# Three of six early weight sums made in y's last places, rings that begin at free buffers, and last loads in places that y has left

## The chip, the cores and the metric

The kernel runs on one NeuronCore of one Trainium2 chip. The metric is the time of one execution on the device, in microseconds (us). Engines are named as in the profile: PE does matmuls and PEld loads their weights beside it, DVE is the vector engine, ACT the scalar engine, POOL the third elementwise engine, and SP issues most of the DMA transfers, in the order in which they stand on its queue.

## The reference, cut to what matters

The input has 256 tokens of 2048 channels. There is one layer (DEPTH is 1), so only the short convolution mixer is computed.

```python
def rmsnorm(x, g):
    y = x * lax.rsqrt(jnp.mean(x * x, axis=-1, keepdims=True) + EPS)
    return y * g

def adaln(h, c, w, b):
    mod = jnp.einsum('bd,df->bf', jax.nn.silu(c), w) + b
    shift, scale, gate = jnp.split(mod, 3, axis=-1)
    return h * (1.0 + scale[:, None, :]) + shift[:, None, :], gate

def short_conv_mixer(h, w_in, conv_w, w_out):      # w_in 2048 x 16384, w_out 4096 x 2048
    proj = jnp.einsum('bsd,de->bse', h, w_in)
    b_gate, c_gate, v, g = jnp.split(proj, 4, axis=-1)
    u = causal_depthwise_conv(c_gate * v, conv_w)   # width 3
    y = b_gate * u * jax.nn.silu(g)
    return jnp.einsum('bse,ed->bsd', y, w_out)

h, gate = adaln(rmsnorm(x, norm_g), c, ada_w, ada_b)
x = x + gate[:, None, :] * short_conv_mixer(h, w_in, conv_w, w_out)
out = rmsnorm(x, final_g)
```

## The kernel before, in words

Everything is float32. A product of two float32 matrices is made of three matmuls on PE: each operand is split into a rounded part `hi` and the rest `lo`, and hi times hi, hi times lo and lo times hi are summed. So every piece of weights goes the same way: a DMA brings it into a buffer `raw`, ACT rounds it into a buffer `hi` (L385), DVE subtracts to make `lo` (L390), and PE multiplies. A piece is 1 MB, 128 partitions of 2048 elements.

The buffers `raw`, `hi` and `lo` are three rings of three buffers each (`w_tile`, L146; `nth` counts where a ring stands). From the second matrix on, each ring has a fourth buffer for a while (`fourth`), a place that held something else before: for `lo` the place b0, for `hi` b1, for `raw` b2, and b2 held a part of `hT`, the normalised input that all matmuls of the first matrix read. A DMA into a buffer waits until the buffer's last reader has ended.

The stages, in the order of time:

- The head and the first half of the first matrix (banks `mm_s`), with the sums of ada_w between them, up to about 377 us.
- The second half of the first matrix (banks `mm_b`, the loop at L787): eight pairs of channel tiles, each by four quarters of two pieces, 64 pieces in all with 48 matmuls each (L550). In some places of this loop a piece of the second matrix is brought in ahead of its time (`early_weights`, L779). The table `EARLY` (L764) says after which piece: six "sums" units at 32, 36, 40, 44, 48 and 52, and two "gated" units at 56 and 60. A unit takes one buffer of the `raw` ring (`raw_u`, loaded at L757) and one of the `lo` ring (`sums_u`). For a sums unit DVE makes four sums of its blocks (L773, 776, 777), and ACT's queue stores the result to DRAM (`made`, L784) one piece later. POOL adds rows of the gate's sums (L719) up to about 610 us.
- The first columns of the second matrix, 16 pairs of row tiles (`first`, L1069). Pairs 8 to 15 go by seven products instead of eight, which need the sums of blocks: those made ahead are read from `made` into `sums_o`, the others are made by DVE here. A raw piece is now loaded into a buffer of the `lo` ring, and its `lo` goes into the `raw` ring, except that the very first piece still loads into the `raw` ring.
- The second columns (`second`), twelve pieces in the order 0, 1, 10, 2, 11, 3, 9, 12, 8, 13, 14, 15, of which 9 to 15 go by seven products. Beside them, the closing loads (`load_ends`, L862) and closing steps of the first columns.
- Four last pieces: the third quarter of the columns for two groups of rows (`third_piece`), and the two gated units read back (`gated_piece`). Then the end: norm, scaling and the store.

From L1063 on, all work stands in the order written, on every engine. In the loop at L787 a scheduler orders the work when the program is built, with some ties set by hand (`add_manual_dep`). `y`, the result between the two matrices, lies in 16 places of a pool of slots, y0 to y15, two channel tiles in each. y14 and y15 are written last.

Of the kernel before, what the change touches and what calls it, by code (L numbers as in the profile page):

```python
# [8 lines left out]
F32 = mybir.dt.float32  # L9
F32R = mybir.dt.float32r  # L10
# [3 lines left out]
P = 128  # L14
# [103 lines left out]
def short_conv_layer(ctx: ExitStack, tc: tile.TileContext, x, c, norm_g, ada_w, ada_b, w_in, conv_w, w_out, final_g, out):  # L118
# [256 lines left out]
    last_low = [None]  # L375

# [6 lines left out]
    def split_hi(raw, n, hi=None):  # L383
        hi = hi_tile() if hi is None else hi
        nc.scalar.copy(hi[:, :n], raw[:, :n])  # L385
        return hi
# [287 lines left out]
    ys.extend(slot([P, 2, 2, T], f"y{j}", F32R) for j in range(len(ys), NCT // 2))  # L674
# [5 lines left out]

    def gate_columns(c0, n):
        if c0 < D // 2:
            return closing[0][:, D // 2 + c0 : D // 2 + c0 + n]
        flat = gate_slots[0].rearrange("p h s f -> p (h s f)").bitcast(F32)
        return flat[:, c0 % 1024 : c0 % 1024 + n]
# [92 lines left out]

    def early_weights():  # L779

        while to_store:
            unit, sums = to_store.pop()
            made[unit] = dram.tile([P, SLOT], F32, tag=f"made{len(made)}", name="made")
            nc.scalar.dma_start(made[unit], sums)  # L784
        unit = EARLY.get(passed[0])
        passed[0] += 1
        if unit is None:  # L787
# [5 lines left out]
        raw, sums = raw_tile("raw_u"), w_tile("lo", "sums_u")  # L793
        blocks, out = (v.rearrange("p (b f) -> p b f", f=W) for v in (raw, sums))
        if unit[0] == "gated":
            load_o(raw, unit[1] * EP, EP, 3 * W, W)
            nc.vector.tensor_tensor(out=out, in0=blocks, in1=turned.unsqueeze(1).to_broadcast([P, EP, W]), op=ALU.mult)
# [64 lines left out]
    def load_ends(n):  # L862
# [20 lines left out]

# [30 lines left out]
    class Columns:  # L914
# [7 lines left out]
        def piece(self, n):  # L922
# [3 lines left out]
            raw = w_tile("raw" if n == 0 and c0 == 0 else "lo", "raw_o")  # L926
            ready = (c0, j) in made
# [26 lines left out]
        def seven(self, j, raw, sums, ready):  # L954
# [10 lines left out]
            opens, last = j == self.in_turn[0], j == self.in_turn[-1]  # L965

# [3 lines left out]
            def products():  # L970
# [3 lines left out]
                triple(p75[:, 0], f(2), sh[:, 1], sl[:, 1], opens, last)  # L974
                triple(p75[:, 1], f(0), sh[:, 0], sl[:, 0], opens, last)
# [43 lines left out]
    def third_piece(ep):  # L1019
        raw = w_tile("lo", "raw_o")  # L1020
        load_o(raw, ep * EP, EP, 2 * W, W)
        return ep, *split(raw, SLOT, "raw")
# [13 lines left out]

    def gated_piece(ep):
        raw = w_tile("lo", "raw_o")
        nc.sync.dma_start(raw, made["gated", ep])
        return raw  # L1040
# [24 lines left out]
    with in_order():  # L1065
# [77 lines left out]
```

## Time and profile before

| | us |
|---|---|
| median of three runs | 902.74 (900.94 to 904.39) |
| the profiled execution | 904.34, of which its span is 902.5 |
| PE busy | 885.8 (98%), clock 0.998 |
| DVE busy | 703.0 (78%) |
| ACT busy | 492.9 (55%) |
| POOL busy | 91.6 (10%) |

A row of the timeline is: start, length, engine and line, operation, what it writes and reads, and in brackets how long the engine stood idle before it and what ended that. A row of the chain of waits is: start, share of the chain, what the chain was doing then. The rows of the DMA view are groups of transfers with their count, their size and the median time from issue to landing. Matmuls overlap in the pipeline, so starts and not lengths say how fast PE goes.

### The profile page before, as it was taken

To read this page: it belongs to the slowest core of one execution; us is meant where nothing else is said; L and a number is where in the kernel's file an instruction comes from. 1 tells how busy PE (TensorE), PEld (TensorE's weight loads), DVE (VectorE), ACT (ScalarE), POOL (GpSimd) and SP (SyncE) were. 2 spreads that over 40 slices of the span, in tenths; PEclk is the share of its full clock that TensorE was granted. 3 is DMA by queue.
4 is the path that set the end of the run, shared out by engine and by line. 5 is a ranking of instruction groups with operands and counts; after the bars stand their busy time and mean duration, and the time that the engine had idled before them with its cause. 6 is when DMAs were issued, how large, how long until landed. Compare 5 with 4: busy or idle time off the path is not lost.

```text
span 902.5 us, 16524 instructions
## 1 busy us (share of the span) xinstructions
PE 885.8 (98%) x6974; PEld 847.6 (94%) x6974; DVE 703.0 (78%) x697; ACT 492.9 (55%) x437; POOL 91.6 (10%) x108
## 2 busy tenths in 40 slices
PE   7999999999999999999999999999999999999996
PEld 4999999999999999999999999999999988888775
DVE  5889988889988867856975687686766589777996
ACT  6767966656558856644343443344434446455553
POOL 0000000010000224420043003310000000000000
PEclk9999999999999999999999999999999999999999
DMA  9999999999998597776877889999998575689672
GB/s 309 367 369 363 366 326 363 332 366 364 373 335 290 164 293 229 240 224 199 284 226 238 256 281 292 312 298 323 299 304 288 197 252 212 195 299 379 235 267 93
DMA packets 165017, 257.29 MB, mean 285 GB/s; under 512 B 7684, under 2 KB 106596, under 8 KB 162896
## 3 DMA queue, kind: packets, MB, share of 16 engines
q1 hardware_dynamic: 159824, 239.89, 80.0%
q0 software_dynamic: 3840, 7.94, 3.2%
q10 hardware_dynamic: 1280, 8.43, 2.3%
q8 instruction: 54, 0.88, 0.4%
q14 instruction: 19, 0.16, 0.0%
HBM read 237.86 MB, written 10.50 MB: 275 GB/s over the span
## 4 chain that ended last, share of the span: by engine, by line
PE 81%; DMA 9%; DVE 6%; ACT 2%; issue 2%; SPq 0%; ACTq 0%; DVEq 0%
PE mm_s L550 39%; PE mm_b L550 27%; PE mm_w L898 7%; PE mm L898 4%; DMA raw<-in_sc_w_in_dram 4%; PE mm_o L898 3%; DVE lo L390 3%; DMA at<-in_ada_w_dram 2%; DMA at_g<-in_ada_w_dram 2%; ACT hi L385 2%; DMA raw_u<-in_sc_w_out_dram 1%; DVE gacc L713 1%; DVE sums_o L773 0%; DVE sums_o L777 0%; DVE sums_o L776 0%
## 5 line engine op out<-in xcount | busy, mean ns | idle before, releaser
L550 PE MATMUL mm_b<-hT,hi 128*128 128x256 f32 x2048 | 348.4, 276 | 0.0
L550 PE MATMUL mm_s<-hT,hi 128*128 128x256 f32 x2048 | 336.3, 277 | 0.0
L550 PEld LDWEIGHTS mm_b<-hT,hi 128*128 128x128 f32 x2048 | 308.2, 188 | 0.0
L550 PEld LDWEIGHTS mm_s<-hT,hi 128*128 128x128 f32 x2048 | 299.7, 188 | 0.2
L550 PE MATMUL mm_b<-hT,lo 128*128 128x256 f32 x1024 | 282.9, 276 | 1.5 <-DVE lo L390 1.5
L550 PE MATMUL mm_s<-hT,lo 128*128 128x256 f32 x1024 | 261.7, 277 | 0.0
L385 ACT CAST hi<-raw 128x2048 fp32r<-128x2048 f32 (+1 forms) x66 | 123.8, 1875 | 187.4 <-PE mm_b L550 88.9
L550 PEld LDWEIGHTS mm_b<-hT,lo 128*128 128x128 f32 x1024 | 192.2, 188 | 1.9 <-DVE lo L390 1.9
L390 DVE TENSOR_TENSOR lo<-raw,hi 128x2048 fp32r<-128x2048 f32 (+1 forms) x66 | 149.4, 2266 | 55.2 <-ACT hi L385 52.9
L550 PEld LDWEIGHTS mm_s<-hT,lo 128*128 128x128 f32 x1024 | 182.7, 188 | 0.0
L390 DVE TENSOR_TENSOR lo<-raw_s,hi 128x2048 fp32r<-128x2048 f32 (+1 forms) x80 | 148.2, 1860 | 29.6 <-ACT hi L385 29.1
L385 ACT CAST hi<-raw_s 128x2048 fp32r<-128x2048 f32 (+2 forms) x81 | 124.1, 1542 | 67.6 <-PE mm_s L550 42.7
L520 DVE SCALAR_TENSOR_TENSOR gv<-at,silu_c,gv 128x512 f32<-128x512 f32 x105 | 78.8, 751 | 9.4 <-DMA at<-in_ada_w_dram 7.5
L573 ACT COPY acc<-mm_s 128x1024 f32<-128x1024 f32 x54 | 54.7, 1012 | 29.6 <-PE mm_s L550 29.5
L719 POOL TENSOR_TENSOR gacc<-gacc,z 128x512 f32<-128x512 f32 x28 | 46.6, 1663 | 113.9 <-DMA z<-gacc 113.9
L898 PE MATMUL mm_w<-hi,y 128*128 128x512 f32 x160 | 52.1, 389 | 0.0
L713 DVE SCALAR_TENSOR_TENSOR gacc<-at_g,silu_c,gacc 128x512 f32<-128x512 f32 x60 | 45.0, 749 | 6.9 <-DMA at_g<-in_ada_w_dram 5.8
L385 ACT CAST hi<-sums_o 128x2048 fp32r<-128x2048 f32 x15 | 28.7, 1910 | 35.6 <-DVE sums_o L777 21.4
L390 DVE TENSOR_TENSOR lo<-raw_o,hi 128x2048 fp32r<-128x2048 f32 x17 | 38.8, 2287 | 11.8 <-PE mm_b L550 6.5
L898 PE MATMUL mm_o<-hi,y 128*128 128x512 f32 x140 | 45.7, 390 | 0.0
L390 DVE TENSOR_TENSOR lo<-sums_o,hi 128x2048 fp32r<-128x2048 f32 x15 | 34.4, 2291 | 12.6 <-ACT hi L385 12.6
L385 ACT CAST hi<-raw_o 128x2048 fp32r<-128x2048 f32 x17 | 32.5, 1909 | 21.0 <-DMA raw_o<-in_sc_w_out_dram 9.2
(188 smaller groups left out, 756.3 us busy)
## 6 DMA issues: line engine op xcount, KB each, us to landing
raw<-in_sc_w_in_dram SPq DMA_DIRECT2D x64, 1024.0 KB, 6.7
raw_s<-in_sc_w_in_dram SPq DMA_DIRECT2D x47, 1024.0 KB, 8.2
at<-in_ada_w_dram SPq DMA_DIRECT2D x126, 256.0 KB, 7.9
raw_o<-in_sc_w_out_dram SPq DMA_DIRECT2D x24, 1024.0 KB, 5.6
raw_s<-in_sc_w_in_dram SPq DMA_DIRECT2D x33, 512.0 KB, 7.4
at_g<-in_ada_w_dram SPq DMA_DIRECT2D x32, 512.0 KB, 8.4
raw_u<-in_sc_w_out_dram SPq DMA_DIRECT2D x8, 1024.0 KB, 5.4
made<-sums_u ACTq DMA_DIRECT2D x8, 1024.0 KB, 7.7
```

What stands on the lines that cost most here:

```text
L385: nc.scalar.copy(hi[:, :n], raw[:, :n])
L390: last_low[0] = nc.vector.tensor_tensor(out=lo[:, :n], in0=raw[:, :n], in1=hi[:, :n].bitcast(F32), op=ALU.subtract)
L520: nc.vector.scalar_tensor_tensor(out=gv, in0=at4[:, i], scalar=c_k, in1=gv, op0=ALU.mult, op1=ALU.add)
L550: mm = last_mm[0] = nc.tensor.matmul(dst, w, h[k], start=begins and left, stop=ends, skip_group_check=True)
L573: nc.scalar.copy(acc[ch, q], bank)
L713: nc.vector.scalar_tensor_tensor(out=ga, in0=at3[:, i, :], scalar=s, in1=ga, op0=ALU.mult, op1=ALU.add)
L719: nc.gpsimd.tensor_tensor(out=ga, in0=ga, in1=turned, op=ALU.add)
L898: nc.tensor.matmul(dst, y[a], b, start=opens and i == 0, stop=ends and i == 2, skip_group_check=True)
```

## The change

- **Units.** The sums for pair 13 of the first columns are no longer made ahead; those for pair 13 of the second columns are. The order of the six is now (0, 15), then 10, 11, 12, 13 and 15 of the second columns.
- **Three of the six in y's last places.** Units 0, 2 and 4 of that list, that is (0, 15), (1024, 11) and (1024, 13), no longer take a buffer of the rings. Each is loaded as two halves of 0.5 MB into the places of y14 and y15, which nothing uses yet. Four DVE operations of 512 columns make the sums in place, tied behind the `lo` of the next piece. Two stores of a half each follow three pieces after the load. Two of the four blocks come out in the other order, and `swapped` reads them so. To make this possible, every slot has its own tag, and y14 and y15 are allocated when they are first written. The other three sums units and the two gated units keep their buffers in the rings.
- **Rings.** At the first raw piece of the second matrix the counts of `raw` and `lo` are set to 0, so that the fourth buffer of `raw` (b2, with hT) is no longer the next one in turn.
- **Places.** x's second half goes to the places of y0 and y1, the gate's second half to that of y10. The third-quarter pieces are loaded as two halves each into y2 and y11, and y3 and y9, with their loads issued at pieces 8 and 11 of the second columns. The gated pieces go to y12 and y8, and y13 and y14. Each half is rounded and subtracted by an instruction of its own. A closing load moves from piece 9 to piece 10, and the closing steps come one piece later from piece 6 on.

```diff
-    slots = ctx.enter_context(tc.tile_pool(name="slots", bufs=NSLOT, side="right"))
-
-    def slot(shape, name, dtype=F32):
-        return slots.tile(shape, dtype, tag="slot", name=name)
+    slots = ctx.enter_context(tc.tile_pool(name="slots", bufs=1, side="right"))
+    taken = [0]
+
+    def slot(shape, name, dtype=F32, at=None):
+        if at is None:
+            at = taken[0] % NSLOT
+            taken[0] += 1
+        return slots.tile(shape, dtype, tag=f"slot{at}", name=name)
...
+    STAGES = 2
+    first_slot = taken[0] - len(ys)
+
+    def y_tile():
+        ys.append(slot([P, 2, 2, T], f"y{len(ys)}", F32R, at=(first_slot + len(ys)) % NSLOT))
+
+    while len(ys) < NCT // 2 - STAGES:
+        y_tile()
+    taken[0] = first_slot + NCT // 2
...
-    UNITS = ((0, 13), (0, 15), (2 * W, 10), (2 * W, 11), (2 * W, 12), (2 * W, 15))
+    UNITS = ((0, 15),) + tuple((2 * W, j) for j in (10, 11, 12, 13, 15))
     EARLY = {32 + 4 * i: unit for i, unit in enumerate(UNITS)}
+    IN_PLACE = UNITS[0:6:2]
     EARLY.update({55: "gate", 56: ("gated", LAST[0]), 60: ("gated", LAST[1])})
     made = {}
-    to_store = []
+    to_do = []
...
+    def sums_in_place(left, right):
+
+        low = last_low[0]
+        b0, b1, b2, b3 = left[:, 0], left[:, 1], right[:, 0], right[:, 1]
+        for out, a, b, op in (
+            (b1, b1, b0, ALU.subtract), (b0, b2, b0, ALU.subtract), (b2, b2, b1, ALU.add), (b3, b3, b2, ALU.subtract)
+        ):
+            step = nc.vector.tensor_tensor(out=out, in0=a, in1=b, op=op)
+            tc.add_manual_dep(step.ins, low.ins.name, after, reason="the blocks are there by then")
+
+    def store_made(unit, parts, turn=None):
+        made[unit] = dram.tile([P, SLOT], F32, tag=f"made{len(made)}", name="made")
+        n = SLOT // len(parts)
+        for i, made_part in enumerate(parts):
+            store = nc.scalar.dma_start(made[unit][:, i * n : (i + 1) * n], made_part)
+            if turn:
+                tc.add_manual_dep(store.ins, turn[0].ins.name, after, reason="the sums are there by then")
...
+        now = passed[0]
         passed[0] += 1
+        for due in [due for due in to_do if due[0] <= now]:
+            to_do.remove(due)
+            due[1](*due[2:])
...
+        if unit[0] == "gated" or unit not in IN_PLACE:
+            raw, result = raw_tile("raw_u"), w_tile("lo", "sums_u")
+            blocks, out = (v.rearrange("p (b f) -> p b f", f=W) for v in (raw, result))
+            if unit[0] == "gated":
+                load_o(raw, unit[1] * EP, EP, 3 * W, W)
+                nc.vector.tensor_tensor(out=out, in0=blocks, in1=turned.unsqueeze(1).to_broadcast([P, EP, W]), op=ALU.mult)
+            else:
+                load_o(raw, 2 * unit[1], 2, unit[0], 2 * W)
+                list(sums_of(blocks, out))
+            to_do.append((now + 1, store_made, unit, [result]))
         else:
-            load_o(raw, 2 * unit[1], 2, unit[0], 2 * W)
-            list(sums_of(blocks, out))
-        to_store.append((unit, sums))
+            c0, j = unit
+            parts = []
+            for i in range(STAGES):
+                parts.append(slot([P, 2 * W], "staged", at=(first_slot + NCT // 2 - STAGES + i) % NSLOT))
+                load = nc.sync.dma_start(parts[i], w_out[0, (2 * j + i) * P : (2 * j + i + 1) * P, c0 : c0 + 2 * W])
+                tc.add_manual_dep(load.ins, last_load[0].ins.name, after, reason="in its turn")
+            to_do.append((now + 1, sums_in_place, *(v.rearrange("p (b f) -> p b f", f=W) for v in parts)))
+            to_do.append((now + 3, store_made, unit, parts, last_high))
...
+                if len(ys) == ct // 2:
+                    y_tile()
...
-                xh.append([slot([P, HD], f"xr{t}") for t in range(TT)])
+                xh.append([y_place(j, f"xr{j}") for j in (0, 1)])
             load_x(1, n - 5)
         elif n == 7:
-            nc.sync.dma_start(gate_columns(HD, HD), gate_row[0:1, HD:D].partition_broadcast(P))
-        elif n == 9:
+            last_gate.append(y_place(10, "last_gate"))
+            nc.sync.dma_start(last_gate[0], gate_row[0:1, HD:D].partition_broadcast(P))
+        elif n == 8:
+            thirds.append(third_load(LAST[0], (2, 11)))
+        elif n == 10:
             load_fg(1)
+        elif n == 11:
+            thirds.append(third_load(LAST[1], (3, 9)))
...
+    def y_place(j, name):
+        return slot([P, 2 * W], name, at=(first_slot + j) % NSLOT)
+
+    def third_load(ep, places):
+        halves_ = [y_place(j, "raw_y") for j in places]
+        for i, raw in enumerate(halves_):
+            load_o(raw, ep * EP + 2 * i, 2, 2 * W, W)
+        return halves_
+
+    def gated_load(ep, places):
+        halves_ = [y_place(j, "raw_y") for j in places]
+        for i, raw in enumerate(halves_):
+            nc.sync.dma_start(raw, made["gated", ep][:, i * 2 * W : (i + 1) * 2 * W])
+        return halves_
+
+    def split_halves(raws):
+        hi, lo = hi_tile(), lo_tile("raw")
+        for i, raw in enumerate(raws):
+            nc.scalar.copy(hi[:, i * 2 * W : (i + 1) * 2 * W], raw)
+        return hi, lo
+
+    def low_halves(raws, hi, lo):
+        for i, raw in enumerate(raws):
+            o = slice(i * 2 * W, (i + 1) * 2 * W)
+            nc.vector.tensor_tensor(out=lo[:, o], in0=raw, in1=hi[:, o].bitcast(F32), op=ALU.subtract)
...
             raw = w_tile("raw" if n == 0 and c0 == 0 else "lo", "raw_o")
+            if n == 0 and c0 == 0:
+                nth.update({"raw": 0, "lo": 0})
...
-            next(steps, None)
+            if n != 6:
+                next(steps, None)
             products()
         assert next(steps, None) is None
-        third0 = third_piece(LAST[0])
+        gated = [gated_load(LAST[0], (12, 8))]
+        third0 = third_piece(LAST[0], thirds[0])
         second.gather()
         third_products(*third0)
-        third_products(*third_piece(LAST[1]))
+        third_products(*third_piece(LAST[1], thirds[1]))
+        gated.append(gated_load(LAST[1], (13, 14)))
         late = []
         for t, ep in enumerate(LAST):
-            raw = gated_piece(ep)
-            hi = split_hi(raw, SLOT)
+            hi, lo = split_halves(gated[t])
             move(t)
-            late.append((ep, *split_lo(raw, SLOT, hi, "raw")))
+            low_halves(gated[t], hi, lo)
+            late.append((ep, hi, lo))
```

The order of the matmuls on PE is the same before and after. Three places of other engines' queues follow. The first is SP's queue at the first early unit (`at_g` is a part of ada_w, `raw` a piece of the first matrix). Before:

```order
L704 DMA at_g<-in_ada_w_dram 128x2x512 x2
L809 DMA raw<-in_sc_w_in_dram 128x8x256
L757 DMA raw_u<-in_sc_w_out_dram 128x2x1024
L809 DMA raw<-in_sc_w_in_dram 128x8x256 x4
L757 DMA raw_u<-in_sc_w_out_dram 128x2x1024
```

Now:

```order
L718 DMA at_g<-in_ada_w_dram 128x2x512 x2
L852 DMA raw<-in_sc_w_in_dram 128x8x256
L841 DMA staged<-in_sc_w_out_dram 128x1024 x2
L852 DMA raw<-in_sc_w_in_dram 128x8x256 x4
L771 DMA raw_u<-in_sc_w_out_dram 128x2x1024
```

The unit keeps its place on the queue. Its one load into the ring has become two loads into places outside the ring.

The second is DVE where the first columns begin, with the last waits of each instruction (PE_49 is a matmul, DMAHW a landing, Activation ACT). The first two rows are the `lo` of the last two pieces of the first matrix. Before:

```order
L390 TENSOR_TENSOR lo_8305<-raw_8301,hi_8303 128x2048 [waits DMAHW1_49,PE_49]
L390 TENSOR_TENSOR lo_8359<-raw_8355,hi_8357 128x2048 [waits DMAHW3_49,DMAHW2_49,Activation_49]
L833 TENSOR_TENSOR z1_4486<-z1_4486 128x512 [waits DVE_49,Activation_49]
L390 TENSOR_TENSOR lo_8433<-raw_o_8429,hi_8431 128x2048 [waits DMAHW4_49,PE_49]
L390 TENSOR_TENSOR lo_8463<-raw_o_8459,hi_8461 128x2048 [waits DMAHW5_49,Activation_49]
L835 TENSOR_TENSOR z1_4486<-mm_b_8300,z1_4486 128x512 [waits DVE_49,PE_49]
```

Now:

```order
L395 TENSOR_TENSOR lo_8313<-raw_8309,hi_8311 128x2048 [waits DMAHW7_49,PE_49]
L395 TENSOR_TENSOR lo_8367<-raw_8363,hi_8365 128x2048 [waits DMAHW1_49,DMAHW0_49,Activation_49]
L395 TENSOR_TENSOR lo_8442<-raw_o_8438,hi_8440 128x2048 [waits DMAHW2_49,DVE_49,Activation_49]
L876 TENSOR_TENSOR z1_4484<-z1_4484 128x512 [waits Activation_49]
L395 TENSOR_TENSOR lo_8472<-raw_o_8468,hi_8470 128x2048 [waits DMAHW3_49,DVE_49,Activation_49]
L878 TENSOR_TENSOR z1_4484<-mm_b_8308,z1_4484 128x512 [waits DVE_49,PE_49]
```

The `lo` of the first piece of the second matrix waited for a matmul. Now it waits for a landing, DVE and ACT, and it stands one instruction earlier.

The third is SP's queue in the second columns, from the gate's second half on (`raw_y` is a third-quarter piece, L931 and L932 are the two raw parts of a pair whose sums are read from `made`, `closing` is final_g). Before:

```order
L880 DMA gate_4483<-gate_row 128x1024
L757 DMA raw_o<-in_sc_w_out_dram 128x2x1024 x2
L857 DMA closing<-in_final_g_dram 128x1024
L757 DMA raw_o<-in_sc_w_out_dram 128x2x1024
L931 DMA raw_o<-in_sc_w_out_dram 128x512
L932 DMA raw_o<-in_sc_w_out_dram 128x1024
L938 DMA sums_o<-made 128x2048
L757 DMA raw_o<-in_sc_w_out_dram 128x4x512 x2
L1039 DMA raw_o<-made 128x2048 x2
```

Now:

```order
L926 DMA last_gate<-gate_row 128x1024
L771 DMA raw_o<-in_sc_w_out_dram 128x2x1024
L771 DMA raw_y<-in_sc_w_out_dram 128x2x512 x2
L1011 DMA raw_o<-in_sc_w_out_dram 128x512
L1012 DMA raw_o<-in_sc_w_out_dram 128x1024
L1018 DMA sums_o<-made 128x2048
L771 DMA raw_o<-in_sc_w_out_dram 128x2x1024
L902 DMA closing<-in_final_g_dram 128x1024
L1011 DMA raw_o<-in_sc_w_out_dram 128x512
L1012 DMA raw_o<-in_sc_w_out_dram 128x1024
L1018 DMA sums_o<-made 128x2048
L771 DMA raw_y<-in_sc_w_out_dram 128x2x512 x2
```

Pair 13 now has three loads of 1.75 MB in all in place of one of 1 MB, and a third-quarter piece of 1 MB stands ahead of them.

More of the change, by code (lines that the diff above doesn't have):

```diff
@@ L384, in split_hi @@
         hi = hi_tile() if hi is None else hi
-        nc.scalar.copy(hi[:, :n], raw[:, :n])
+        last_high[0] = nc.scalar.copy(hi[:, :n], raw[:, :n])
         return hi
@@ L777, in sums_of @@
         yield nc.vector.tensor_tensor(out=s[:, 3], in0=b[:, 3], in1=s[:, 2], op=ALU.subtract)
-    def early_weights():
[L781 to L785, printed above, removed]
+    def sums_in_place(left, right):
[13 more added lines that the diff above has]
+                tc.add_manual_dep(store.ins, turn[0].ins.name, after, reason="the sums are there by then")
+    def early_weights():
+        now = passed[0]
         passed[0] += 1
+        for due in [due for due in to_do if due[0] <= now]:
+            to_do.remove(due)
+            due[1](*due[2:])
+        unit = EARLY.get(now)
         if unit is None:
@@ L792, in early_weights @@
             return
[L793 to L797, printed above, removed]
-        else:
-            load_o(raw, 2 * unit[1], 2, unit[0], 2 * W)
-            list(sums_of(blocks, out))
-        to_store.append((unit, sums))
+        if unit[0] == "gated" or unit not in IN_PLACE:
[8 more added lines that the diff above has]
+            to_do.append((now + 1, store_made, unit, [result]))
+        else:
+            c0, j = unit
[6 more added lines that the diff above has]
+            to_do.append((now + 3, store_made, unit, parts, last_high))
     for ct in range(NS, NCT, 2):
@@ L973, in products @@
                 triple(bank(0, 0), f(3), bh[:, 2], bl[:, 2])
-                triple(p75[:, 0], f(2), sh[:, 1], sl[:, 1], opens, last)
-                triple(p75[:, 1], f(0), sh[:, 0], sl[:, 0], opens, last)
+                triple(p75[:, 0], f(2), sh[:, 1 - swapped], sl[:, 1 - swapped], opens, last)
+                triple(p75[:, 1], f(0), sh[:, swapped], sl[:, swapped], opens, last)
                 triple(p6, f(1), sh[:, 2], sl[:, 2], opens, last)
@@ L1017, in out_mm, with third_piece @@
             triple(bank, y_parts(ep * EP + i, t), hi[:, o], lo[:, o], False, ep == LAST[-1] and i == EP - 1)
[L1019 to L1022, printed above, removed]
+    def third_piece(ep, raws):
+        hi, lo = split_halves(raws)
+        low_halves(raws, hi, lo)
+        return ep, hi, lo
     def third_products(ep, hi, lo):
@@ L1035, in move @@
         nc.scalar.copy(po[t], c)
[L1037 to L1040, printed above, removed]
     def third(t):
```

8 lines of the change are left out of this document (5 added, 3 removed).

## The prediction

> **What bounds the kernel now.** I read the page first, then the busy times by stage, then PE's timeline for each place where it stood, and last the chain of waits behind each of those places.
>
> ```profile
> PE 885.8 (98%) x6974; PEld 847.6 (94%) x6974; DVE 703.0 (78%) x697; ACT 492.9 (55%) x437; POOL 91.6 (10%) x108
> ```
>
> PE works for 98% of the span. The order of its matmuls does not change, so the change can win only time in which PE stands still. The busy times (columns: PE, PEld, DVE, ACT, POOL, clock, DMA share, GB/s) say where that is:
>
> ```profile
> core 0: us, PE busy (x) PEld busy (x) DVE busy (x) ACT busy (x) POOL busy (x), PEclk, DMA share, GB/s
> 545.00:612.00 67.00, 65.45 (x574) 65.06 (x574) 48.38 (x43) 27.51 (x21) 20.37 (x20) 1.00 0.96 306
> 612.00:705.00 93.00, 93.00 (x823) 93.00 (x823) 60.83 (x54) 38.40 (x29) 0.00 (x0) 1.00 0.91 299
> 728.40:770.00 41.60, 41.60 (x183) 34.44 (x184) 40.09 (x33) 22.01 (x14) 0.00 (x0) 1.00 0.63 215
> 837.00:866.00 29.00, 27.71 (x119) 21.25 (x117) 27.65 (x21) 16.97 (x12) 0.00 (x0) 1.00 0.73 255
> 866.00:895.40 29.40, 29.32 (x128) 23.93 (x128) 26.17 (x31) 14.31 (x18) 0.00 (x0) 1.00 0.41 154
> ```
>
> The clock is 1.00 everywhere. PE misses 1.5 us at 545 to 612, 1.3 us at 837 to 866, and next to nothing elsewhere. The stalls themselves, in brackets the idle time and its releaser:
>
> ```profile
> 562.98 0.39 PE L550 MATMUL mm_b<-hT,lo 128*128 128x256 f32 x1 [0.76 <-DVE lo L390]
> 607.60 0.39 PE L550 MATMUL mm_b<-hT,lo 128*128 128x256 f32 x1 [0.79 <-DVE lo L390]
> 728.39 0.50 PE L898 MATMUL mm_w<-lo,y 128*128 128x512 f32 x1 [0.79 <-DVE lo L390]
> 852.13 0.50 PE L898 MATMUL mm_o<-lo,y 128*128 128x512 f32 x1 [0.32 <-DVE lo L390]
> 863.31 0.50 PE L898 MATMUL mm<-lo,y 128*128 128x512 f32 x1 [0.65 <-DVE lo L962]
> 865.98 0.50 PE L898 MATMUL mm<-lo,form_g 128*128 128x512 f32 x1 [0.32 <-DVE lo L390]
> ```
>
> A stall costs more than its bracket, since the pipeline drains and refills. PE's pace without waits is in the chain of waits:
>
> ```profile
> 377.03 125.02 PE mm_b L550 x1103
> 872.88 11.56 PE mm_o L898 x51
> ```
>
> That is 0.1133 us a matmul of 256 columns and 0.227 us one of 512. Starts around a stall then lie about 0.27 us further apart than the bracket says. So the stalls cost 1.03 and 1.06 (A, in the first matrix), 1.06 (B, where the second matrix begins), and 0.59, 0.92 and 0.59 (C, in the second columns). C has some 0.3 us more in gaps without a bracket, 2.4 in all. Together 5.5 us: the most that can be won. Every one of them waits for a `lo` of DVE.
>
> **A: the first matrix.** Its stalls lie behind long loads, as the chain shows:
>
> ```profile
> 550.48 11.11 DMA raw<-in_sc_w_in_dram
> 561.68 1.92 ACT hi L385
> 563.62 2.31 DVE lo L390
> 577.40 9.71 DMA raw<-in_sc_w_in_dram
> ```
>
> and SP's timeline shows when an early unit and the piece behind it were issued, and DVE's what the unit makes:
>
> ```profile
> 538.33 0.37 SPq L757 DMA_DIRECT2D raw_u<-in_sc_w_out_dram  x1
> 544.10 6.74 SPq L809 DMA_DIRECT2D raw<-in_sc_w_in_dram  x3
> 563.00 0.37 SPq L757 DMA_DIRECT2D raw_u<-in_sc_w_out_dram  x1
> 546.79 1.22 DVE L773 TENSOR_TENSOR sums_u<-raw_u 128x1024 f32<-128x1024 f32 x1
> 548.05 1.67 DVE L776 TENSOR_TENSOR sums_u<-raw_u,sums_u 128x512 f32<-128x512 f32 x1
> 549.75 0.69 DVE L777 TENSOR_TENSOR sums_u<-raw_u,sums_u 128x512 f32<-128x512 f32 x1
> ```
>
> The DMA view of 545 to 612 and of 612 to 705 gives the loads (median to landing):
>
> ```profile
> raw<-in_sc_w_in_dram SPq DMA_DIRECT2D x12, 1024.0 KB, 9.0
> raw<-in_sc_w_in_dram SPq DMA_DIRECT2D x18, 1024.0 KB, 7.1
> ```
>
> A turn of a `raw` buffer is load, hi and lo: 9.0 + 1.92 + 2.31 = 13.2 us. A piece lasts 48 x 0.1133 = 5.44 us. With one unit to four pieces, three buffers serve five loads in 21.8 us, so a turn may last 3 x 21.8 / 5 = 13.1 us: no slack, and PE stalls. From 612 on, with POOL at rest, a turn is 7.1 + 4.2 = 11.3, and there are no stalls. Where a unit stays out of the ring, a turn may last 3 x 5.44 = 16.3. The first stall lies in the group of unit 0 (issued at 538.33), the second 44.6 us later, two groups on, in that of unit 2. These are two of the three units that leave the ring. The piece behind the unit (544.10) no longer waits for one more buffer, and can be issued up to one piece, 5.4 us, sooner.
>
> Against it stands that no byte goes away: with the DMA engines 96% busy, a load that is issued sooner may only wait longer. I take 1.6 of 2.1 us, with bounds 0 (loads land when they did) and 2.1.
>
> The sums in place cost DVE four times 0.69 instead of 1.22 + 0.69 + 0.69, 0.16 us more a unit, and 0.5 us for three. DVE is busy for 60.83 of 93 us there, so this is hidden. It would cost 0.5 if that cover were gone. Behind the first matrix's `lo` they also let that `lo` go ahead of them. The doubled loads and stores stand on SP and ACT (0.37 us an issue, ACT 38.40 of 93 busy): nothing. y14 waits for the stores of the last unit, which are sent five pieces, 27 us, before y14 is written: nothing.
>
> The Trainium skill ("DMA: Bandwidth & Descriptors", section "Bandwidth") asks for transfers of at least 1 MiB, and its section "Anatomy of one DMA — SWDGE (gpsimd) path" gives about 2.0 us fixed beside the bytes, for a queue that these loads don't use. By it the three extra loads would be an estimated 6 us of DMA time, and the first rival below would come true. The backlog under C, where transfers of different sizes keep above 400 GB/s, speaks for overlap of that fixed part.
>
> **B: where the second matrix begins.**
>
> ```profile
> 726.05 4.49 DVE L390 TENSOR_TENSOR lo<-raw_o,hi 128x2048 fp32r<-128x2048 f32 x2 [6.51 <-PE mm_b L550]
> ```
>
> DVE stood 6.51 us with its source long there, because its target lies on hT, and began when the last matmul of the first matrix had ended. PE then had only hi products to do. In the order of the change this `lo` waits for a landing, DVE and ACT. All of these lie well before 726, so it is done early. It gains 1.06, with the lower bound 0 (the first load would wait for another buffer that is as late). I take 1.0.
>
> The sums of pair 13 come back into the first columns: 2.60 us of DVE at about 780. DVE is nearly full at 728 to 770 (40.09 of 41.6), but there it has room:
>
> ```profile
> 782.21 2.29 DVE L390 TENSOR_TENSOR lo<-sums_o,hi 128x2048 fp32r<-128x2048 f32 x1 [4.11 <-ACT hi L385]
> ```
>
> The 4.11 us gap takes them: nothing, or 2.6 if the pairs there had no lead.
>
> **C: the second columns.** DVE is the bound behind the stalls (27.65 of 29 us):
>
> ```profile
> 849.79 2.29 DVE L390 TENSOR_TENSOR lo<-raw_o,hi 128x2048 fp32r<-128x2048 f32 x1
> 851.99 1.22 DVE L773 TENSOR_TENSOR sums_o<-raw_o 128x1024 f32<-128x1024 f32 x1
> ...
> 854.58 1.75 DVE L962 TENSOR_TENSOR lo<-raw_o,hi 128x1536 fp32r<-128x1536 f32 x1
> 856.71 2.29 DVE L390 TENSOR_TENSOR lo<-sums_o,hi 128x2048 fp32r<-128x2048 f32 x1 [0.38 <-ACT hi L385]
> 858.92 1.22 DVE L773 TENSOR_TENSOR sums_o<-raw_o 128x1024 f32<-128x1024 f32 x1
> ```
>
> The 2.60 us at 851.99 (pair 13) go. In their place its sums must land. SP's timeline, and the DMA view of 837 to 870 (slices of 0.83 us):
>
> ```profile
> 841.08 3.06 SPq L757 DMA_DIRECT2D raw_o<-in_sc_w_out_dram  x2
> 848.76 0.37 SPq L757 DMA_DIRECT2D raw_o<-in_sc_w_out_dram  x1
> GB/s 278 407 437 382 343 0 89 213 407 432 358 422 417 422 387 99 194 343 382 209 55 20 0 0 79 201 258 415 179 417 328 268 79 82 298 407 412 308 385 390
> raw_o<-in_sc_w_out_dram SPq DMA_DIRECT2D x5, 1024.0 KB, 5.4
> ```
>
> A backlog moves about 420 GB/s, 2.5 us a MB. Behind pair 8's load (841.08, landing by 846.5) now come a third-quarter piece of 1 MB, pair 13's raw parts of 0.75 MB and its sums of 1 MB: 2.75 x 2.5 = 6.9 us, so the sums land at 853.4. Then hi (1.92) and lo (2.29) of them end at 857.6 instead of 859.0, and what follows on DVE comes 1.4 us sooner. If the sums must instead wait for a buffer until 848.76, where pair 14's load had its one, they land at 854.3 and the chain gains 0.5. A third-quarter piece has shorter rows; the two in the trace landed so:
>
> ```profile
> DMA to landing us min/median/max: 5.4/5.9/6.4
> ```
>
> That is up to 1.0 more than the 5.4 of the others. With it the gains are 0.4 and -0.5. Bounds -0.5 and 1.4. I take 0.7, nearer to the case without any late buffer, since pair 14's load had its one early.
>
> The last four pieces are split by halves: two times 1.22 on DVE in place of 2.29, 0.15 us each. At 866 to 895 DVE has 26.17 of 29.4 us and PE stands still for 0.1, so 0.6 us more fits, and their raws now land earlier, in places free for long. Closing steps one piece later: the same work, 0.
>
> **The sum.** Profiled execution: 904.34 - 1.6 - 1.0 - 0.7 = 901.0. This execution is 1.6 above the median, and the fastest run is 3.4 below it. The stalls of A hang on landings, and I suppose that a median run has about three quarters of them. So A counts 1.2, and the forecast is 902.74 - 1.2 - 1.0 - 0.7 = **899.8**.
>
> **The rivals.**
>
> - *Loads land when they did* (A gains nothing). For it speaks the DMA share of 0.96. Against it speaks that both stalls lie in groups whose unit leaves the ring. 902.74 - 1.0 - 0.7 = 901.0. Chance 0.22.
> - *All stalls go.* For it speaks that all six have one releaser, DVE's `lo`, and the change works on each. Against it speaks the 27.65 of 29 us, from which only 2.6 are taken. 902.74 - 1.5 - 1.06 - 2.4 = 897.8. Chance 0.15.
> - *A new wait at pair 13: slower.* SP is in order. If the buffer for pair 13's sums comes free only when DVE has ended pair 8's `lo` (852.0), the sums land about 5.4 us later, at 857.5. Their lo then ends at 861.7 instead of 859.0, and pair 14 behind them is as late: 2.7 us lost. With A at 0 and B at 1.0 the time is 902.74 - 1.0 + 2.7 = 904.4. It decides for slower once the sums land more than about 2 us after 854.8, where they were ready before. Against it speaks that pair 14's load had its buffer at 848.76. Chance 0.13.
> - *The change doesn't do what it says*, in that the first `lo` still waits for a late matmul: B falls away, 900.8. It is within the forecast's own range, and its chance with it.
>
> **How the numbers follow.** The forecast keeps 0.50, with its own range 898.3 to 901.3. The range over the cases is 897.0 to 903.0, which leaves out most of the slower case and the end of the best. A measurement of this kernel can tell about 0.5%, 4.5 us, from no change. Faster by more needs 898.2 or less: most of the second rival and a small part of the forecast, 0.17. Slower by more needs 907.3, beyond every priced case: 0.03. Same: 0.80.
>
> **What would show it.** A: the brackets at about 563 and 607 are gone, and the piece behind a staged unit is issued 5 us sooner. B: no idle time of DVE before the first `lo` of raw_o ended by a matmul. C: pair 13's `sums_o` lands by 853 to 854 on this clock (3 us sooner on the new one), and PE's brackets at pairs 8, 13 and 14 shrink from 2.4 us to about 1.7. PE's count and pace stay. The prediction is wrong if PE shows a new bracket of over 1 us, above all in pairs 13 to 15, or at pair 13 of the first columns, or if B's bracket stands.

## The result: 908.62 us, and the profile after

The change made the kernel slower. Its median is 908.62 us over 12 runs (901.13 to 916.04), against 902.76 for the kernel before over 12 runs (900.94 to 904.39). The ratio is 1.0052, with a 95% interval of 1.0031 to 1.0074; it leaves out one disturbed run of the twelve. 899.8 was predicted, with a range up to 903.0. The profiled execution took 909.11, its span is 907.3.

The runs of the kernel before lie within 3.5 us of each other, the eleven of the change within 10.6 (901.13 to 911.68). So the change added something that differs from one execution to the next. The busy times of the stages, which answer to those shown of before (same columns):

```profile
430.00:470.00 40.00, 36.66 (x313) 35.67 (x312) 35.20 (x30) 13.70 (x11) 14.00 (x16) 1.00 0.77 233
530.00:560.00 30.00, 27.10 (x233) 26.51 (x232) 24.66 (x23) 10.58 (x8) 6.47 (x7) 1.00 0.93 297
560.00:612.00 52.00, 52.00 (x461) 52.00 (x460) 37.40 (x39) 22.57 (x17) 13.70 (x15) 1.00 1.02 315
841.00:871.00 30.00, 28.95 (x126) 23.01 (x125) 27.12 (x19) 17.68 (x12) 0.00 (x0) 1.00 0.91 336
```

PE now stands still for 3.3 us at 430 to 470 and for 2.9 at 530 to 560. Before, it had no stall at all between 377 and 561, as most of this stretch shows:

```profile
377.00:545.00 168.00, 168.00 (x1485) 168.00 (x1484) 120.64 (x116) 71.58 (x56) 30.17 (x35) 1.00 0.78 243
```

The two stalls of A, at 563 and 607.6 before, would lie 8.4 us later here, at about 571 and 616. From 555 to 867 PE's timeline has no bracket, so both are gone. The brackets that it does show are these (there are four more, of 0.41 us or less, among the new ones):

```profile
438.32 0.39 PE L555 MATMUL mm_b<-hT,lo 128*128 128x256 f32 x1 [1.25 <-DVE lo L395]
451.29 0.38 PE L555 MATMUL mm_b<-hT,lo 128*128 128x256 f32 x1 [1.08 <-DVE lo L395]
536.19 0.39 PE L555 MATMUL mm_b<-hT,lo 128*128 128x256 f32 x1 [1.80 <-DVE lo L395]
548.46 0.38 PE L555 MATMUL mm_b<-hT,lo 128*128 128x256 f32 x1 [1.08 <-DVE lo L395]
867.70 0.50 PE L976 MATMUL mm<-lo,y 128*128 128x512 f32 x1 [0.71 <-DVE lo L1042]
870.37 0.50 PE L976 MATMUL mm<-lo,form_g 128*128 128x512 f32 x1 [0.33 <-DVE lo L395]
```

Counted from start to start, as in the prediction, the new stalls cost 4.7 us (five, at 437 to 463) and 3.7 us (three, at 535 to 554). They have the releaser that was expected, DVE's `lo`, but not the cause. The same piece of DVE's timeline, of before and of after, gives the cause of the first five. Before:

```profile
425.23 0.68 DVE L754 TENSOR_TENSOR gate<-z,gate 128x512 fp32r<-128x512 f32 x1
425.84 0.48 DVE L711 TENSOR_SCALAR gacc<-at_g,silu_c 128x512 f32<-128x512 f32 x1
426.35 1.54 DVE L713 SCALAR_TENSOR_TENSOR gacc<-at_g,silu_c,gacc 128x512 f32<-128x512 f32 x2
427.91 2.29 DVE L390 TENSOR_TENSOR lo<-raw,hi 128x2048 fp32r<-128x2048 f32 x1
```

After:

```profile
425.99 0.68 DVE L768 TENSOR_TENSOR gate<-z,gate 128x512 fp32r<-128x512 f32 x1
432.88 0.49 DVE L725 TENSOR_SCALAR gacc<-at_g,silu_c 128x512 f32<-128x512 f32 x1 [6.21 <-DMA gate_row<-gacc]
433.40 2.67 DVE L727 SCALAR_TENSOR_TENSOR gacc<-at_g,silu_c,gacc 128x512 f32<-128x512 f32 x2
435.98 2.28 DVE L395 TENSOR_TENSOR lo<-raw,hi 128x2048 fp32r<-128x2048 f32 x1
```

The order is the same, row by row. But the first sum of the gate's third block now waits 6.21 us, and the `lo` behind it comes 8 us later than it did. `gacc` is the block's running sum. It has two buffers. A block's buffer comes back when POOL has folded it over the partitions and stored it to `gate_row`. The waits of POOL between 200 and 400 us say why the fold ends late. Before:

```profile
POOL z L717 <- DVE acc L630: 72.3, 1, 72.3
```

After:

```profile
POOL z L731 <- DVE acc L636: 151.5, 1, 151.5
```

The fold loads its rows into the first half of `z0`. Before, its first load started at 304.9 us, now it starts at 384.2. It waits for another instruction of DVE, on another tile that lay in z0's place. With one tag per slot the places go in turn, and z0 lies on a sum of the last channel group, which is read until 384 us. In the kernel before, z0 came to lie on a sum of the second group; the pool seems to have given each new tile a place that had come free. This is read from the instruction that each wait ends with. The order of instructions does not show it, since it is a matter of addresses.

SP shows the second half of the damage. Its queue after:

```profile
425.50 0.37 SPq L852 DMA_DIRECT2D raw<-in_sc_w_in_dram  x1
435.31 0.37 SPq L718 DMA_DIRECT2D at_g<-in_ada_w_dram  x1
438.30 0.37 SPq L852 DMA_DIRECT2D raw<-in_sc_w_in_dram  x1
```

A part of ada_w (`at_g`) waits until DVE has used up an earlier one, whose buffer it takes, and the next piece of weights stands behind it: 12.8 us between two loads of weights, where a piece of work takes 5.44.

The three stalls at 535 to 554 have no such wait in front of them. There DVE stands for landings of `at_g`, first for 2.71 us and then four times more, for 0.74 to 2.12 us each, between one `lo` and the next:

```profile
521.34 0.49 DVE L725 TENSOR_SCALAR gacc<-at_g,silu_c 128x512 f32<-128x512 f32 x1 [2.71 <-DMA at_g<-in_ada_w_dram]
```

The kernel before has such waits there too (2.35, 0.31 and 3.85 us), without a stall of PE. That these three stalls also come from the late folds is therefore not read from this profile; the experiments below bear on it.

### The profile page after: what moved, and what is told of

It reads as the page before. It is cut to its first block, busy times and chain, and to the rows that moved or that the text cites. A ratio compares the mean times of both kernels' runs of the same rounds, so it can differ in the third digit from the quotient of the medians.

```text
span 907.3 us, 16555 instructions
## 1 busy us (share of the span) xinstructions
PE 887.0 (98%) x6974; PEld 848.6 (94%) x6974; DVE 702.0 (77%) x704; ACT 493.0 (54%) x441; POOL 93.8 (10%) x108
## 4 chain that ended last, share of the span: by engine, by line
PE 79%; DMA 10%; DVE 5%; issue 3%; ACT 2%; POOL 2%; SPq 0%; ACTq 0%; DVEq 0%; POOLq 0%
PE mm_s L555 39%; PE mm_b L555 25%; PE mm_w L976 7%; PE mm L976 4%; DMA at_g<-in_ada_w_dram 3%; PE mm_o L976 3%; DMA z<-gacc 3%; DMA at<-in_ada_w_dram 2%; DVE lo L395 2%; ACT hi L390 1%; POOL gacc L733 1%; DVE gacc L727 1%; DMA sums_o<-made 1%; DMA gate_row<-gacc 1%; POOL z L731 0%
## 5 line engine op out<-in xcount | busy, mean ns | idle before, releaser
L395 DVE TENSOR_TENSOR lo<-raw,hi 128x2048 fp32r<-128x2048 f32 (+1 forms) x66 | 151.9, 2305 | 61.9 <-ACT hi L390 59.3
L727 DVE SCALAR_TENSOR_TENSOR gacc<-at_g,silu_c,gacc 128x512 f32<-128x512 f32 x60 | 49.1, 818 | 8.9 <-DMA at_g<-in_ada_w_dram 7.8
L592 ACT COPY mm_s<-acc 128x1024 f32<-128x1024 f32 x38 | 38.6, 1016 | 2.5 <-DVE acc L581 1.8
L395 DVE TENSOR_TENSOR lo<-raw_o,hi 128x2048 fp32r<-128x2048 f32 x13 | 29.7, 2289 | 10.5 <-ACT hi L390 10.5
```

The costliest lines, as they stand in the source:

```text
L395: last_low[0] = nc.vector.tensor_tensor(out=lo[:, :n], in0=raw[:, :n], in1=hi[:, :n].bitcast(F32), op=ALU.subtract)
L592: nc.scalar.copy(bank, acc[ch, q])
L727: nc.vector.scalar_tensor_tensor(out=ga, in0=at3[:, i, :], scalar=s, in1=ga, op0=ALU.mult, op1=ALU.add)
```

## The experiments

Each run was measured beside the kernel before on the same chip. That one took 902.79 us beside the runs on tags alone, z0 early, the old ring and units in the rings, 903.11 beside the two with four buffers and the two tied ones, and 903.75 beside the two that move the third-quarter piece and the reset alone.

### One tag per slot, alone

To the kernel before, only this was done:

```diff
-    slots = ctx.enter_context(tc.tile_pool(name="slots", bufs=NSLOT, side="right"))
+    slots = ctx.enter_context(tc.tile_pool(name="slots", bufs=1, side="right"))
+    taken = [0]
...
-        return slots.tile(shape, dtype, tag="slot", name=name)
+        taken[0] += 1
+        return slots.tile(shape, dtype, tag=f"slot{(taken[0] - 1) % NSLOT}", name=name)
```

> The kernel before with one edit: every slot gets its own tag, taken in turn, as the change does. The order of the work on all engines stays that of before; only places move, and the first half of z0, into which the gate's folds are loaded, comes to lie on a sum of the last channel group, which DVE reads until about 384 us, instead of one that is free at 305. Theory (the fold's place): POOL's first fold starts at about 380 instead of 305, folds run late into the second half of the first matrix, PE shows new stalls between 430 and 560, and the time is 905 to 909. Rival (the halved loads and stores in y's last places crowd the DMA engines): there are none here, so the time stays at 902.8 within 1 us.

Measured: 913.01 us (909.67 to 917.88), ratio 1.0113 (1.0083 to 1.0143). The rival falls: there is no halved load in this kernel, and it is slower than the whole change. In the two traces each of the five engines has the same instructions in the same order as before, so only places differ. POOL's wait is 151.5 us again, and DVE waits 10.4 us for the row of the gate:

```profile
POOL z L719 <- DVE acc L633: 151.5, 1, 151.5
...
DVE gacc L713 <- DMA gate_row<-gacc: 10.4, 1, 10.4
...
PE mm_b L552 <- DVE lo L392: 4.6, 1, 4.6
```

It is also slower than the theory's 905 to 909. The profile is that of the slowest of the six executions (917.88), and it shows two reasons. One is that PE's stall of 4.64 us is followed by 4.6 us at half the clock:

```profile
441.00:446.00 5.00, 4.77 (x23) 4.77 (x24) 4.89 (x6) 0.00 (x0) 2.51 (x3) 0.51 0.72 204
```

23 matmuls in 4.8 us instead of 42: the drop costs another 2.1 us. The other is that the stalls of A, which this kernel still has, came out longer here (2.20 and 1.75 us, in place of 0.76 and 0.79), and that the clock fell to half once more behind the first of them, which cost 1.6 us (the rows are in the last section). Together, the new stalls (7.2 us from start to start), the half clock (2.1 and 1.6) and the longer stalls of A (2.4) make 13.3 us: from 904.34 to 917.6, against 917.88 measured.

### z0 in a place that is free early

In the change, z0 and y11 exchange places:

```diff
+    def y_at(j):
+        return (first_slot + (18 if j == 11 else j)) % NSLOT
...
-    zs = [slot([P, 2, 2, T], f"z{j}") for j in range(2)]
+    zs = [slot([P, 2, 2, T], f"z{j}", at=(first_slot + (11, 19)[j]) % NSLOT) for j in range(2)]
```

> The changed kernel with one edit: the places of z0 and y11 are exchanged, so that z0 lies on a sum that is free at about 305 us. Theory (the fold's place): POOL folds from 305 us on, the stalls at 436 to 463 (4.9 us) and at 534 to 554 (3.7 us) go, and the profiled time falls from 909.1 to about 900.5, that is 2 us faster than before. Rival (halved loads): the stalls stay and the time stays at 906 to 909.

Measured: 910.01 us (908.71 to 910.67), ratio 1.0070 (1.0051 to 1.0090). POOL's first fold starts after 72.3 us of waiting again, and all eight new stalls are gone. But the time is no better, and neither side had expected that. DVE's timeline and the clock show it:

```profile
355.91 0.48 DVE L728 TENSOR_SCALAR gacc<-at_g,silu_c 128x512 f32<-128x512 f32 x1 [12.64 <-DMA gate_row<-gacc]
```

```profile
362.00:367.00 5.00, 5.00 (x24) 5.00 (x25) 4.89 (x5) 0.00 (x0) 2.31 (x3) 0.51 0.98 317
```

In this kernel the scheduler put the third block's first sum in front of the last pieces of the first half of the first matrix, 70 us sooner than before. The store of the fold that it needs landed at 355.9, so DVE waited 12.64 us, PE 6.45, and PE went on at half the clock. So the wait for a buffer of `gacc` is the cause, and z0's place is only one of two ways into it: the fold may be late, or the sum may be early.

### The same, with four buffers of gacc

The third and fourth block's sums get buffers of their own, in places of y that are not written yet:

```diff
         if j == 0:
-            gacc[0] = adap.tile([P, 512], F32, tag="gv", name="gacc")
+            if dc < 2:
+                gacc[0] = adap.tile([P, 512], F32, tag="gv", name="gacc")
+            else:
+                gacc[0] = slot([P, 512], "gacc", at=(first_slot + 10 + dc) % NSLOT)
```

> As the run with z0 early, but the gate's third and fourth blocks of sums get buffers of their own, in the places of y12 and y13, so that DVE never waits for a fold of POOL to give back a buffer of sums. The scheduler then puts the loads of the third block three pieces of weights ahead of the second half of the first matrix. Theory (DVE stands at the first sum of a block until a fold ends, and the lo behind it is late): the stall of 6.4 us at 355 and the half clock behind it go, and the time falls from 910.0 to 900 to 902. Rival (folds and ada loads crowd the DMA engines): the stalls only move, and the time stays above 905.

Measured: 899.57 us (899.00 to 903.61, 12 runs), ratio 0.9965 (0.9953 to 0.9977): faster than the kernel before, and within 0.3 us of what was predicted for the change. PE has no stall between 200 and 800 us:

```profile
340.00:380.00 40.00, 40.00 (x355) 40.00 (x355) 39.15 (x39) 24.31 (x26) 14.60 (x16) 1.00 0.86 268
430.00:470.00 40.00, 40.00 (x355) 40.00 (x355) 22.40 (x20) 17.52 (x14) 13.17 (x14) 1.00 0.72 221
545.00:612.00 67.00, 67.00 (x594) 67.00 (x593) 48.69 (x47) 27.66 (x21) 18.04 (x20) 1.00 0.96 298
```

The last row is the stage in which PE was busy for 65.45 of 67 us before. The piece behind the first staged unit is issued at 537.49 us instead of 544.10, and the loads of that stage land after 8.8 us (median), where it was 9.0.

### Four buffers of gacc, with z0 where the change puts it

> The same own buffers for the third and fourth blocks of sums, with z0 left where the change puts it, so POOL's first fold still starts at about 384 us. The order of every engine is that of the run before. Theory (the place of z0 hurts only through the wait of DVE for a buffer of sums): within 1.5 us of that run, 900 to 903. Rival (late folds load the DMA engines when the first matrix has no slack): the stalls between 530 and 610 stay and the time is 3 us or more above it.

Measured: 902.49 us (898.99 to 904.15, 12 runs), ratio 0.9990 (0.9979 to 1.0001). POOL still waits 151.5 us. With nothing but two more buffers the change's 908.62 falls by 6.1 us. But the median is 2.9 us above the run with z0 early and four buffers, nearly the 3 that the rival asked for. The profiled execution was the fastest of the twelve and has no stall between 200 and 850 us, so the three stalls at 535 to 554 went with the two buffers there. In other executions late folds may cost something besides that wait; where, no profile here shows, and it stays open.

### The third block tied to its old time

With z0 early and two buffers of gacc, the first sum of the third block is tied behind a later `lo`:

```diff
             if j + i == 0:
-                nc.vector.tensor_scalar_mul(ga, at3[:, i, :], s)
+                first = nc.vector.tensor_scalar_mul(ga, at3[:, i, :], s)
+                if dc == 2:
+                    tc.add_manual_dep(first.ins, last_low[0].ins.name, after, reason="the fold is done by then")
```

> As the run with z0 early, with two buffers of sums, but the first sum of the third block is tied on DVE behind the lo of piece 16 of the second half (about 460 us), when the fold of the first block has long ended. Theory: no wait of DVE for a fold at the start of that block, the stall of 6.4 us goes, and of the change only its own gains are left: 902.8 - 2.1 - 1.1 - 0.8 = 898.8, at most 901. Rival (the wait wasn't the order but the folds' length): a wait of DVE for the landing of a gate row comes back at the fourth block, and the time is above 904.

Measured: 900.58 us (899.25 to 903.45, 12 runs), ratio 0.9974 (0.9963 to 0.9985). That is 9.4 us less than the same kernel without the tie. No wait of DVE for a gate row is left. In its profile the third fold runs from 480 to 532 us, almost as late as in the change (486 to 534), without a stall of PE; so a late fold alone does not make the stalls at 535 to 554. It is 1.8 us above the 898.8 hoped for, and within the bound of 901. Both cures, more buffers or a later sum, work on the same wait, and both give about what the prediction said of the change.

### The parts of the change, one by one

**B, the rings.** The kernel with z0 early, without the reset of the counts:

> As the run with z0 early, but the ring counts are not set to 0 at the first piece of the second matrix. If step B of the prediction is right, PE shows again a bracket of 0.8 us at the first lo of that piece, ended by a matmul on DVE's side, and the time is 1.0 us above the run with z0 early. If another wait stood behind it, the two are equal.

Measured: 911.11 us (909.49 to 912.88), 1.1 above the run with z0 early. The times of the two overlap, so the difference alone is not clear of noise; but the bracket is back as it was:

```profile
736.27 0.50 PE L979 MATMUL mm_w<-lo,y 128*128 128x512 f32 x1 [0.79 <-DVE lo L395]
```

The reset alone, in the kernel before:

```diff
             raw = w_tile("raw" if n == 0 and c0 == 0 else "lo", "raw_o")
+            if n == 0 and c0 == 0:
+                nth.update({"raw": 0, "lo": 0})
```

> The kernel before with one edit: the ring counts are set to 0 at the first piece of the second matrix. Step B of the prediction says 1.0 us less, 901.8 to 902.1, with no bracket at the first lo of that piece. A rival says that the wait is moved to the next buffer, and the time stays.

Measured: 902.29 us (12 runs), ratio 0.9987 (0.9972 to 1.0002), about 1.2 us less, with an interval that just reaches no change. The bracket is gone from its profile. That execution was the slowest of the twelve (907.21) by other stalls, above all the first of A (2.13 us in place of 0.76) and half the clock behind it, so its span says nothing of B.

**A, units outside the rings.** The kernel with z0 early and `IN_PLACE = ()`:

> As the run with z0 early, but all six sums units take buffers of the rings, as before; nothing is loaded into y's last places. If step A is right, stalls of about 1 us each come back between 545 and 612 and the time is 1.6 to 2.1 us above the run with z0 early. If loads land no sooner for it, the two are equal.

Measured: 912.12 us (910.28 to 912.56), 2.1 above. The stalls are back where they were:

```profile
572.00 0.39 PE L555 MATMUL mm_b<-hT,lo 128*128 128x256 f32 x1 [1.68 <-DVE lo L395]
...
616.35 0.39 PE L555 MATMUL mm_b<-hT,lo 128*128 128x256 f32 x1 [0.54 <-DVE lo L395]
```

**C, the units' list.** The tied kernel with the six units of before:

> As the tied run, but with the early units of before: (0, 13) is made ahead and the sums of pair 13 of the second columns are made in the second columns again. If step C is right that the 2.60 us of sums set the end there, PE's brackets in pairs 8, 13 and 14 grow again and the time is 0.7 us above the tied run (0.4 to 1.4). If the loads in their place cost as much, the two are equal.

Measured: 901.02 us (10 runs), 0.4 above the tied kernel, with ratios of 0.9977 (0.9967 to 0.9986) and 0.9974 (0.9963 to 0.9985): not told apart by the times. In the profiles the brackets are 1.83 us with the old list and 1.06 with the new, of which the one at pair 14 carries most of the difference (old list, then new):

```profile
858.62 0.50 PE L981 MATMUL mm<-lo,y 128*128 128x512 f32 x1 [1.22 <-DVE lo L1047]
```

```profile
857.88 0.50 PE L981 MATMUL mm<-lo,y 128*128 128x512 f32 x1 [0.73 <-DVE lo L1047]
```

### Where pair 13's sums stand on SP's queue

In the tied kernel the chain of waits names what still bounds the second columns:

```profile
840.78 8.44 DMA sums_o<-made
849.23 0.02 issue
...
849.33 1.92 ACT hi L390
...
853.48 1.23 DVE sums_o L793
```

These are pair 13's sums, 8.44 us on their way behind the third-quarter piece. To the kernel with four buffers of gacc, two runs move that piece back:

```diff
-        elif n == 8:
+        elif n == 9:
             thirds.append(third_load(LAST[0], (2, 11)))
```

> As the run with z0 early and four buffers of sums, but the first third-quarter piece (1 MB) is issued behind pair 13's three loads instead of ahead of them. If step C is right that pair 13's sums land late because of it, they land about 2.5 us sooner, DVE no longer waits for them, PE's last two brackets (0.65 and 0.30) shrink, and the time falls by 0.5 to 1.4 us to about 898.6. If DVE's own work is the bound, the time stays within 0.3 us.

Measured: 900.05 us (10 runs), ratio 0.9959 (0.9946 to 0.9972). The sums land at 848.10 instead of 850.41. Of these 2.3 us, 0.9 is there before the moved piece: pair 8's load, which stands ahead of both, was already issued at 836.79 instead of 837.72. So the move brought 1.4 us, less than the 2.5 expected. And now pair 14's load comes behind the piece, lands at 853.52, and DVE waits for it:

```profile
853.61 1.23 DVE L794 TENSOR_TENSOR sums_o<-raw_o 128x1024 f32<-128x1024 f32 x1 [1.17 <-DMA raw_o<-in_sc_w_out_dram]
```

Of PE's last two brackets 0.86 us are left, from 0.95. So the wait has passed to the next transfer. The second run issues the piece at n = 10, behind pair 14's load and the closing load too:

> The same, with that piece also behind pair 14's load and the closing load. If pair 14's landing is the next bound, it comes 2.5 us sooner too and the time is a further 0.3 to 0.8 us lower, 898.0 to 898.6. If DVE is the bound by then, it is equal to the run before. If the piece itself is now late, PE shows a bracket at the first matmul of the third quarter.

Measured: 899.62 us (7 runs), ratio 0.9957 (0.9941 to 0.9973). Only the last bracket, 0.34, is left in its profile:

```profile
860.89 0.50 PE L981 MATMUL mm<-lo,form_g 128*128 128x512 f32 x1 [0.34 <-DVE lo L395]
```

Its ratio is the lowest of all, but the three intervals (0.9965, 0.9959, 0.9957) overlap. The profiles say up to 0.9 us, the times do not settle it.

## Why the prediction was wrong

**The step that failed** is in the costs put at nothing. The prediction prices the units, the rings and the moved loads, and says of the places only that the raws lie "in places free for long". One tag per slot was taken as a means for y14 and y15. Nobody asked which tile every other slot tile now lies on. The mechanism it left out is worth +8.4 us in the profiled execution: 4.7 us behind DVE's wait for a buffer of `gacc`, which the profile shows, and 3.7 us in three later stalls, which go with it in the runs but whose own path stays open. Alone, on the kernel before, one tag per slot costs 10.2 us (1.13%).

**The sum closes with it.** From the profiled 904.34, less A (2.1), B (1.1) and C (0.7), plus the new stalls (8.4), comes 908.8, against 909.11 measured. A, B and C are there, in the change itself: no stall from 555 to the second matrix, no bracket where the second matrix begins, and 1.8 us of gaps instead of 2.5 in the second columns.

- **A** was priced at 1.6 in the profiled execution and 1.2 in the median. The undoing of it cost 2.1. The objection that loads issued sooner only land later (the first rival) is refuted.
- **B** was priced at 1.0 and measured 1.1 by its undoing, and about 1.2 alone. Neither time is clear of noise by itself; what shows B is the bracket that comes and goes.
- **C** was priced at 0.7, and the profile of the change shows 0.7. The places differ: the gaps at pairs 8 and 13 shrank, but the bracket at pair 14 stayed (0.71 after 0.65), because pair 13's sums land late behind the third-quarter piece. The DMA backlog was read nearly rightly: the sums were to land 12.3 us behind the issue of pair 8's load (841.08 to 853.4), and in the change they landed 12.8 us behind it (846.28 to 859.06).
- **The slower rival** had the right sign and the wrong place. It looked for the new wait at pair 13 of the second columns; it was at the gate's third block, 400 us earlier, with a price three times as high.
- **The median.** That a median run has three quarters of A was a supposition. With the wait for `gacc` cured, the median is 899.57 or 900.58. By the ratios this is 3.2 or 2.3 us less than the kernel before, where 2.9 was predicted, so the sum was near what the rest of the change is worth.
- The last section of the prediction named a new bracket of over 1 us as what would prove it wrong, and named three places. Such brackets came (1.08 to 1.80 us), but at none of these places.

The row that could have warned stood in the profile before: POOL waited 72.3 us for an `acc` of DVE before its first fold. That says that z0's place decides when folds begin, and so that z0's next place had to be looked up.

## What to carry to other kernels

Where a change alters how a pool hands out buffers, list for every tile which tile lies under it before and after, and when that one is last read; the order of instructions does not show it. An engine that works in order passes any wait on, so look for the small side job (here a fold on POOL, 10% busy) whose late end holds a buffer that the busy engine needs. And a profile whose stalls end at the expected releaser is not yet explained: read what that releaser itself had waited for.

## What the runs showed of the hardware

After PE had stood still for 4.64 us (one tag per slot) and 6.45 us (z0 early), it ran for 4.6 and 5.1 us at a granted clock of about 0.5. A matmul of 256 columns then came every 0.213 us instead of every 0.113, so that half the clock cost about 2.1 and 2.3 us on top of the stall. Much shorter stalls did the same. These rows stand behind a stall of 2.20 us in the run with one tag per slot, and behind one of 2.13 us in the run with the reset alone:

```profile
575.60:579.00 3.40, 3.40 (x19) 3.40 (x18) 2.80 (x1) 1.79 (x2) 2.36 (x3) 0.50 0.86 310
563.95:567.36 3.41, 3.41 (x18) 3.41 (x18) 2.29 (x1) 1.45 (x2) 1.26 (x1) 0.50 0.83 247
```

In each, half the clock lasted 3.4 us and cost about 1.6. After stalls of 1.80 us (the change), 1.75 (one tag per slot) and 1.68 (units in the rings) the clock stayed at full speed. So a stall of a little over 2 us cost nearly twice its own length here.

The Trainium skill ("TensorE: Matmul & The Clock Gate", section "Part 1: The HAM clock gate") says that the clock halves after an idle window of about 3.4 us and comes back after as long a busy one. The 3.4 us of the way back agree with the two rows; the idle window does not, since 2.13 and 2.20 us of idle time were enough here.

This may be part of why the runs of the change lie so far apart: the mean clock was 0.993 and 0.995 in the runs of 910.15 and 911.68 us, and 0.996 to 0.999 in the nine faster ones. These runs had no profile, so that is not shown.
